# Down weights split by a converting and an adding transfer, and one weight sum of the seven products by an adding one

## The chip, the cores and the metric

The kernel runs on one NeuronCore of one Trainium2 chip. The metric is the device time of one launch in microseconds; lower is better. Five engines work side by side, each through its own queue, in order: TensorE (PE; its weight loads are listed as PEld), VectorE (DVE), ScalarE (ACT), GpSimd (POOL) and SyncE (SP). SP and POOL issue transfers, which run on 16 DMA engines.

## What is computed

A decoder trunk of two layers over 512 tokens and 16 learned ones, with 1024 features, in float32:

```
h = concat(meta, x)
for l in range(2):
    h = layer_norm(ALPHA * h + 0.5 * swiglu(h, ffn1_w_up[l], ffn1_w_down[l]))
    h = layer_norm(ALPHA * h + hybrid_mixer(h, ...))
    h = layer_norm(ALPHA * h + 0.5 * swiglu(h, ffn2_w_up[l], ffn2_w_down[l]))
return h[:, N_META:]

def swiglu(x, w_up, w_down):
    gate, up = jnp.split(x @ w_up, 2, axis=-1)      # 2 x 2816 columns
    return (jax.nn.silu(gate) * up) @ w_down
```

The mixer (a short convolution and an attention, gated) is not touched by the change.

## The kernel before

Each float32 product is made of three passes of a shorter format, float32r. An operand is split into hi (its value rounded to 12 significant bits) and lo (the exact rest); hi\*hi, hi\*lo and lo\*hi are summed in PSUM (`mm3`, lines 90 to 93). Weights are the stationary operand in up products and in most down products. So every tile of weights (128 x 1024 values, 512 KB) takes three steps ahead of its matmuls: SP loads it into a raw tile (`load`, line 105), ScalarE casts it to hi (line 111), and DVE subtracts to get lo (line 114). Line 111 and line 114 are in `operand`, which all weights share.

The pools that matter: `raw` has four buffers for raw tiles, `wp` four pairs hi and lo, and each feed-forward has a pool of its own (`dp` or `fp` in the code) with two buffers for raw tiles and two pairs hi and lo. A load waits until the last reader of its buffer is through.

There are four feed-forwards. Each starts with `up_start` (four tiles of features by plain products), which also makes four combinations of the tokens' parts (`combos`: POOL subtracts in line 337, ScalarE and DVE split in line 88). Then `up_seven` runs nine times, 36 times in the whole kernel. It makes two tiles of gate and two of up by seven products of halves, 24 matmuls each, in the order M1, M6, gate A, M7, M4, M5, M3. It reads four blocks of weights: g1, u1 and g2 into `raw`, u2 into the feed-forward's own pool, and makes further operands of them on DVE: S1 = u1 + u2 (line 431, into a tile of the own pool, where u2 lies too), S3 = g1 - u1 in u1's place (432), S2 = S1 - g1 in g1's place (433), S4 = g2 - S2 (441). M6 takes S2, M7 takes S3, M4 takes u2, M5 takes S1 and M3 takes S4, the last split in two halves on DVE. Products that share a bank of PSUM add to it: M6, M7 and M4 use one pair, and DVE reads it in between (lines 436, 446, 450); M5 and M3 use another (460, 468).

After M6 and after M5 stands one step of down products each (`steps`, line 498; two steps in the chunk that has one pair). A step makes one tile of down weights an operand in the feed-forward's own pool, where the two pairs hi and lo take turns, and multiplies it by the earlier chunk's activations for both halves of the tokens. DVE adds the results to the residual (line 558 in the first chunk, then 564, and 599 in the last feed-forward). In the first chunk of a feed-forward, DVE also converts the first features of each half of the tokens (line 253) and TensorE takes their mean (line 254, `shift_by`), which POOL subtracts (line 561). The weights of the last chunk go through `last_units` and not through `steps`.

The order of the instructions on an engine is not that of the source: in the trace, the sums and splits of the next `up_seven` stand between those of the present one, so that operands lie ready well ahead of their products.

Of the kernel before, what the change touches and what calls it, by code (L numbers as in the profile page):

```python
# [18 lines left out]
P = 128  # L19
# [18 lines left out]
# token ranges (first, width): all tokens, and those behind the meta tokens  # L38
FULL = ((0, 256), (256, 272))
TRIM = ((16, 256), (272, 256))  # L40
# and in two equal parts
EVEN = {FULL: ((0, 264), (264, 264)), TRIM: TRIM}
# chunks of the feed-forward features, in pairs of tiles
# [8 lines left out]
def trunk(ctx: ExitStack, tc: tile.TileContext, x, meta, f1_up, f1_dn, w_in, b_gate, conv_w, qn_g, w_uq,  # L52
          kvn_g, w_ukv, w_bc, w_bm, w_o, f2_up, f2_dn, ln_g, ln_b, rope, out):
    """Float32 products run as three passes of float32r: an operand is hi + lo, hi its value rounded to 12
    significant bits and lo the exact rest, and hi*hi + hi*lo + lo*hi are summed in PSUM. Activations lie with
    their features on the partitions."""
# [8 lines left out]
    @contextmanager  # L65
    def scratch(n, t):
        """The eight banks of PSUM, n for psum() and the others for psum2(), and t tiles in SBUF."""
        with tc.tile_pool(name="psp", bufs=1, space=bass.MemoryType.PSUM, reuse_waits="tile") as pool, \
                tc.tile_pool(name="tmp", bufs=t, reuse_waits="tile") as tp:
            banks.append((pool, n))  # L70
            tps.append(tp)
            yield
            banks.pop()
            tps.pop()
# [23 lines left out]
    def unit(pool=wp, k=8, c=P):  # L98
        """A stationary operand, hi and lo, as [128, k, c]."""
# [8 lines left out]
    def operand(raw, pool=wp, cut=1):  # L108
        """Split, in parts where others would wait for long."""
# [6 lines left out]

    def columns(src, c, pool=wp):
        """128 columns of a matrix with 1024 rows."""
        return operand(load(src[:, c:c + P], KD, P), pool)

# [10 lines left out]
    # per-feature parameters as columns  # L131
# [11 lines left out]
    def tokens_in(xt, c0):  # L143
        """Two tiles of tokens, to the columns from c0."""
# [14 lines left out]
    with tc.tile_pool(name="xload", bufs=1, reuse_waits="tile") as xp, scratch(4, 1):  # L159
# [8 lines left out]
        # the array's clock falls while it waits for the first products' operands: of no use but for that  # L168
# [3 lines left out]
    def rest_in(pool):  # L172
        """The other tokens, and the parameters."""
# [21 lines left out]
    # Per-token statistics are taken with the tokens on the partitions, n of them in each of nt columns, and  # L195
    # spread back over the partitions of the features.
# [5 lines left out]
    def token_sums(ps, at, parts, n, nt):  # L202
        """Columns at, at + 2, ...: the means over D features of the parts together."""
# [6 lines left out]
    def spread(c, n, nt, act, ps):  # L210
        """c / D on all partitions."""
# [10 lines left out]
    def rsqrt(v, n, nt, by=float(D)):  # L222
        """by/sqrt(v): the exponent trick, a Newton step, and a step of third order."""
# [13 lines left out]
    class Norm:  # L237
        """Layer norm over the features of r, which holds twice the sum to norm. The sums of r and of its squares
        are taken as its last parts come; by then r has been moved by a value near the mean of each token, which
        keeps the variance exact."""  # L240
# [7 lines left out]
        def shift_by(self, q0, w, i):  # L248
            """The mean of the first features of each token, on all partitions: near the mean, so that a rounded
            one does."""  # L250
# [22 lines left out]
        def run(self, q0, w):  # L273
            """The rest, in steps between which the tensor engine should have something else to do."""
# [44 lines left out]
    def project_steps(ps, u, nk, rhs, q0, w, n=4):  # L319
        """The same, with a stop after each n of the products' parts."""  # L320
# [7 lines left out]
    def combos(hv, th, tl):  # L328
        """Sums and differences of the parts of x (halves of its features, 1 and 2, and of its tokens, A and B)
        that the seven products take, split, from r that holds x. By index: T1 = x1B - x1A,  # L330
        T2 = x2B - T1, T3 = x2B - x1B, -T4 = x2A - T2."""
# [8 lines left out]
    def up_start(hp, dp, w_up, hv, pending, th, tl, after, begin):  # L340
        """silu(gate) * up for the first two pairs of feature tiles. What the first tokens allow comes first."""
# [857 lines left out]
```

## Time and profile before

| | |
|---|---|
| time, median of 3 runs | 2246.11 us (2245.96 to 2246.87) |
| span of the profiled execution | 2247.7 us |
| TensorE busy | 2202.0 us (98%) |
| DVE, ScalarE, POOL busy | 1679.5, 974.5, 372.6 us |
| TensorE clock granted, mean | 0.990 |
| transfers by SP's queue, by POOL's | 195.65 MB, 4.34 MB |

The span is that of one execution, from its first to its last instruction; no other time of that execution is given, so it is compared with the median of the runs. Busy time of an engine is time in which it has an instruction; idle time before an instruction is put down to what released it.

### The profile page before, as it was taken

To read this page: it belongs to the slowest core of one execution; us is meant where nothing else is said; L and a number is where in the kernel's file an instruction comes from. 1 tells how busy PE (TensorE), PEld (TensorE's weight loads), DVE (VectorE), ACT (ScalarE), POOL (GpSimd) and SP (SyncE) were. 2 spreads that over 40 slices of the span, in tenths; PEclk is the share of its full clock that TensorE was granted. 3 is DMA by queue.
4 is the path that set the end of the run, shared out by engine and by line. 5 is a ranking of instruction groups with operands and counts; after the bars stand their busy time and mean duration, and the time that the engine had idled before them with its cause. 6 is when DMAs were issued, how large, how long until landed. Compare 5 with 4: busy or idle time off the path is not lost. (4 is left out here: it accounts for less than half of the span.)

```text
span 2247.7 us, 43950 instructions
## 1 busy us (share of the span) xinstructions
PE 2202.0 (98%) x17989; PEld 2181.9 (97%) x17989; DVE 1679.5 (75%) x3191; ACT 974.5 (43%) x1881; POOL 372.6 (17%) x487
## 2 busy tenths in 40 slices
PE   9999999999999999999999999999999999999998
PEld 8999999999999999999999999999999999999998
DVE  6777778876646777878778778787665568877887
ACT  4343344465533543434353433444655335443441
POOL 3210004211014512000242100042110155100000
PEclk9999999999999999999999999999999999999999
DMA  5232232222233223323323232322222332233322
GB/s 172 94 103 91 90 119 77 68 62 67 69 92 104 66 82 98 113 75 111 107 66 95 96 98 90 113 85 63 66 67 76 94 94 85 76 103 105 99 90 86
DMA packets 237418, 202.80 MB, mean 90 GB/s; under 512 B 6990, under 2 KB 233360, under 8 KB 237216
## 3 DMA queue, kind: packets, MB, share of 16 engines
q1 hardware_dynamic: 234880, 195.65, 28.2%
q0 software_dynamic: 2336, 4.34, 0.7%
q8 instruction: 141, 2.31, 0.4%
q14 instruction: 61, 0.50, 0.1%
HBM read 195.74 MB, written 2.10 MB: 88 GB/s over the span
## 5 line engine op out<-in xcount | busy, mean ns | idle before, releaser
L114 DVE TENSOR_TENSOR wl<-raw,wh 128x1024 fp32r<-128x1024 f32 (+1 forms) x490 | 560.5, 1145 | 250.0 <-ACT wh L111 248.5
L111 ACT CAST wh<-raw 128x1024 fp32r<-128x1024 f32 (+1 forms) x454 | 466.2, 1034 | 591.2 <-PE ps L92 174.3
L92 PE MATMUL ps<-xl,wh 128*128 128x256 f32 (+2 forms) x1760 | 501.7, 285 | 2.7 <-DVE xl L88 2.7
L91 PE MATMUL ps<-xh,wh 128*128 128x256 f32 (+2 forms) x1760 | 502.5, 286 | 0.1
L93 PE MATMUL ps<-xh,wl 128*128 128x256 f32 (+2 forms) x1760 | 501.6, 285 | 0.0
L92 PEld LDWEIGHTS ps<-xl,wh 128*128 128x128 f32 x1760 | 332.5, 189 | 4.3 <-DVE xl L88 4.0
L91 PEld LDWEIGHTS ps<-xh,wh 128*128 128x128 f32 x1760 | 333.0, 189 | 0.6 <-ACT xh L88 0.5
L93 PEld LDWEIGHTS ps<-xh,wl 128*128 128x128 f32 x1760 | 333.4, 189 | 0.0
L91 PE MATMUL ps<-th,wh 128*128 128x264 f32 (+1 forms) x1152 | 328.5, 285 | 0.0
L92 PE MATMUL ps<-tl,wh 128*128 128x264 f32 (+1 forms) x1152 | 327.6, 284 | 0.0
L93 PE MATMUL ps<-th,wl 128*128 128x264 f32 (+1 forms) x1152 | 326.9, 284 | 0.0
L91 PE MATMUL pf<-hh,wh 128*128 128x256 f32 (+1 forms) x864 | 246.7, 286 | 0.0
L93 PE MATMUL pf<-hh,wl 128*128 128x256 f32 (+1 forms) x864 | 246.3, 285 | 0.0
L92 PE MATMUL pf<-hl,wh 128*128 128x256 f32 (+1 forms) x864 | 245.3, 284 | 0.0
L92 PEld LDWEIGHTS ps<-tl,wh 128*128 128x128 f32 x1152 | 218.8, 190 | 0.0
L91 PEld LDWEIGHTS ps<-th,wh 128*128 128x128 f32 x1152 | 218.6, 190 | 0.1
L93 PEld LDWEIGHTS ps<-th,wl 128*128 128x128 f32 x1152 | 218.3, 189 | 0.0
L91 PE MATMUL pf<-xh,wh 128*128 128x256 f32 (+1 forms) x640 | 188.0, 294 | 0.0
L92 PE MATMUL pf<-xl,wh 128*128 128x256 f32 (+1 forms) x640 | 184.4, 288 | 0.0
L93 PE MATMUL pf<-xh,wl 128*128 128x256 f32 (+1 forms) x640 | 183.2, 286 | 0.0
L91 PEld LDWEIGHTS pf<-hh,wh 128*128 128x128 f32 x864 | 162.7, 188 | 0.0
L93 PEld LDWEIGHTS pf<-hh,wl 128*128 128x128 f32 x864 | 162.7, 188 | 0.0
(323 smaller groups left out, 4870.3 us busy)
## 6 DMA issues: line engine op xcount, KB each, us to landing
raw<-in_ffn_w_up_dram SPq DMA_DIRECT2D x176, 512.0 KB, 3.6
raw<-in_ffn_w_down_dram SPq DMA_DIRECT2D x80, 512.0 KB, 3.3
raw<-in_mix_w_in_dram SPq DMA_DIRECT2D x64, 512.0 KB, 3.7
raw<-in_w_o_dram SPq DMA_DIRECT2D x16, 512.0 KB, 3.9
raw<-in_ffn_w_down_dram SPq DMA_DIRECT2D x16, 256.0 KB, 2.6
raw<-in_w_br_conv_dram SPq DMA_DIRECT2D x8, 512.0 KB, 3.3
raw<-in_w_br_mla_dram SPq DMA_DIRECT2D x8, 512.0 KB, 3.3
out_dram<-r SPq DMA_DIRECT2D x8, 256.0 KB, 2.4
```

What stands on the lines that cost most here:

```text
L91: PE.matmul(ps, lhsT=lhs[0], rhs=rhs[0], start=first, stop=False, skip_group_check=more)
L92: PE.matmul(ps, lhsT=lhs[0], rhs=rhs[1], start=False, stop=False, skip_group_check=more)
L93: PE.matmul(ps, lhsT=lhs[1], rhs=rhs[0], start=False, stop=last, skip_group_check=more)
L111: S.copy(u[0], raw)
L114: V.tensor_tensor(u[1][:, k:k + n], raw[:, k:k + n], u[0][:, k:k + n].bitcast(F32), op=ALU.subtract)
```

## The change

Down weights of `steps` no longer have a raw tile. POOL issues a transfer straight from DRAM that converts float32 to float32r into hi; ScalarE writes -hi into lo; POOL issues a second transfer of the same weights from DRAM that adds to lo. This holds for 80 tiles, 64 of 512 KB and 16 of 256 KB. In `up_seven`, S1 is made by a load of u1's block into S1's buffer (SP) and a transfer from u2 that adds to it (POOL), in place of DVE's line 431. The rest of the diff takes out comments.

```diff
+    def operand_dma(src, kc, cols, pool=wp):
+        u = unit(pool, kc, cols)
+        src = src.rearrange("(k p) c -> p k c", p=P)
+        G.dma_start(u[0], src)
+        S.activation(u[1], u[0].bitcast(F32), AF.Copy, scale=-1.0)
+        G.dma_start(u[1], src, accum_op=ALU.add)
+        return u
...
-        s1 = raw_tile(fp).rearrange("p (k c) -> p k c", c=256)
-        V.tensor_tensor(s1, u1, u2, op=ALU.add)          # S1
+        s1 = load(w_up[0:512, D_FF + f * P:D_FF + f * P + 256], KH, 256, fp)
+        G.dma_start(s1, u2, accum_op=ALU.add)
...
+            def weights_dma(ci, mp, pool):
+                f0, f1 = [2 * c for c in CHUNKS[ci]]
+                return operand_dma(w_dn[f0 * P:f1 * P, mp * 256:(mp + 1) * 256], f1 - f0, 256, pool)
...
-                        u = by_tile(operand(weights(ci, mp, rawp), dp), len(hs))
+                        u = by_tile(weights_dma(ci, mp, dp), len(hs))
```

## Rows read from the trace of the kernel before

**Rows 1.** The page, part 1: busy us, share of the span, instructions.

```profile
PE 2202.0 (98%) x17989; PEld 2181.9 (97%) x17989; DVE 1679.5 (75%) x3191; ACT 974.5 (43%) x1881; POOL 372.6 (17%) x487
```

**Rows 2.** Busy times by stretch; last columns PEclk, DMA share, GB/s; sum of four stretches.

```profile
1945.00:2200.00 255.00, 255.00 (x2165) 255.00 (x2164) 201.19 (x336) 100.97 (x157) 0.00 (x0) 1.00 0.30 96
sum 985.00, PE 985.00 PEld 984.82 DVE 769.73 ACT 385.94 POOL 33.47; mean PE 246.25 PEld 246.20 DVE 192.43 ACT 96.48 POOL 8.37
```

**Rows 3.** Timeline of PE, three stretches: start, duration, instruction, idle before, releaser.

```profile
79.84 0.41 PE L254 MATMUL ps<-t,onesb 128*128 128x272 bf16 x1 [2.67 <-DVE t L253]
...
829.84 0.29 PE L254 MATMUL ps<-t,onesb 128*128 128x272 bf16 x1 [2.38 <-DVE t L253]
...
1204.57 0.29 PE L254 MATMUL ps<-t,onesb 128*128 128x272 bf16 x1 [2.21 <-DVE t L253]
```

**Rows 4.** Busy times in slices of 1 us behind the second of these.

```profile
830.00:831.00 1.00, 1.00 (x7) 1.00 (x7) 0.00 (x0) 0.66 (x2) 0.37 (x1) 0.59 0.00 0
831.00:832.00 1.00, 1.00 (x7) 1.00 (x6) 0.20 (x1) 1.00 (x2) 1.00 (x2) 0.50 0.00 0
...
833.00:834.00 1.00, 1.00 (x8) 1.00 (x7) 0.46 (x2) 0.00 (x0) 0.00 (x0) 0.71 0.00 0
```

**Rows 5.** Timeline of DVE before the second stop of rows 3.

```profile
818.22 2.35 DVE L114 TENSOR_TENSOR wl<-raw,wh 128x1024 fp32r<-128x1024 f32 x2
...
822.76 0.29 DVE L253 CAST t<-r 128x256 bf16<-128x256 f32 x1
825.67 1.22 DVE L431 TENSOR_TENSOR raw<-raw 128x1024 f32<-128x1024 f32 x1 [2.62 <-DMA raw<-in_ffn_w_up_dram]
...
827.14 1.22 DVE L432 TENSOR_TENSOR raw<-raw 128x1024 f32<-128x1024 f32 x1
...
828.97 0.81 DVE L253 CAST t<-r 128x272 bf16<-128x272 f32 x1
```

**Rows 6.** Timeline of SP: the last of four loads, there and in a later `up_seven`.

```profile
820.61 0.37 SPq L105 DMA_DIRECT2D raw<-in_ffn_w_up_dram  x1
...
168.87 0.37 SPq L105 DMA_DIRECT2D raw<-in_ffn_w_up_dram  x1
```

**Rows 7.** DMA issues: count, KB each, median us from issue to landing.

```profile
raw<-in_ffn_w_down_dram SPq DMA_DIRECT2D x80, 512.0 KB, 3.3
...
wh<-in_ln_g_dram POOLq DMA_DIRECT2D x1, 512.0 KB, 3.9
wl<-in_ln_b_dram POOLq DMA_DIRECT2D x1, 512.0 KB, 5.2
```

**Rows 8.** Timeline of POOL: a transfer that it issues.

```profile
389.81 0.57 POOL L691 DMA_DIRECT2D cosT<-in_rope_dram  x1
```

**Rows 9.** Timeline of PE: gate A, M7, M3 and the next first step's product begin.

```profile
175.21 0.28 PE L91 MATMUL ps<-xh,wh 128*128 128x264 f32 x1
178.12 0.28 PE L91 MATMUL ps<-th,wh 128*128 128x264 f32 x1
...
192.71 0.28 PE L91 MATMUL ps<-xh,wh 128*128 128x264 f32 x1
...
201.47 0.28 PE L91 MATMUL pf<-hh,wh 128*128 128x256 f32 x1
```

**Rows 10.** Timeline of ACT in the same `up_seven`: two of its casts of weights.

```profile
178.25 1.05 ACT L111 CAST wh<-raw 128x1024 fp32r<-128x1024 f32 x1 [1.00 <-PE ps L92]
...
184.36 2.00 ACT L111 CAST wh<-raw 128x1024 fp32r<-128x1024 f32 x2 [2.16 <-DMA raw<-in_ffn_w_down_dram]
```

**Rows 11.** Timeline of DVE in the same `up_seven`.

```profile
179.34 0.69 DVE L114 TENSOR_TENSOR wl<-raw,wh 128x512 fp32r<-128x512 f32 x1 [3.42 <-ACT wh L111]
179.94 0.43 DVE L446 TENSOR_TENSOR t<-ps,t 128x264 f32<-128x264 f32 x1
...
183.72 1.22 DVE L433 TENSOR_TENSOR raw<-raw 128x1024 f32<-128x1024 f32 x1
...
187.40 0.77 DVE L460 TENSOR_TENSOR t<-ps,t 128x264 f32<-128x264 f32 x2
```

## The prediction

> **What bounds the kernel now.** I read first the page's busy times: TensorE is busy 2202.0 of the span's 2247.7 us [rows 1], so an edit that gives no matmul less can win 45.7 us at most. Then the busy times by stage: in the middle of the four feed-forwards (985 us together) TensorE is busy all the time at full clock, with DVE busy for 201.2 us of the 255 in the stretch shown [rows 2]. That is where nearly all of the edited instructions stand, so relief of DVE buys nothing there, whatever it amounts to.
>
> Third, TensorE's timeline, for the idle time that the edit can reach. In three of the four feed-forwards TensorE stops once, in the first `up_seven`, before the second matmul of `shift_by` (line 254): 2.67, 2.38 and 2.21 us, released by DVE's line 253 [rows 3]. After each the granted clock stands at its lower level, 1.2 GHz instead of 2.4: 0.59, 0.50, 0.50 (the slice not shown is like 831) and 0.71 in four 1-us slices, which loses 0.41 + 0.50 + 0.50 + 0.29 = 1.70 us of full-clock time [rows 4]; the other two have the same pattern. The fourth feed-forward has no `shift_by`. DVE's timeline shows why line 253 is late: after the first one (822.76 to 823.05) DVE waits 2.62 us for a load of `w_up`, does line 431 (the sum S1) for 1.22 us, and only then the rest: 432, the residual's 558, and 253 at 828.97 [rows 5]. The load was issued as the last of four on SP's queue, at 820.61 [rows 6], right after the two splits on DVE that began at 818.22 and took 2.35 us [rows 5]; so its buffer was freed by the second of them. In a later `up_seven` the last of the four is likewise issued at 168.87 [rows 6]. `u2` and S1 share the feed-forward's own pool of two, the others lie in the pool of four; I take the last load to be `u2`.
>
> **The change, part by part.**
>
> *S1 (36 times).* DVE loses line 431: 36 x 1.22 us [rows 5]. At the three stops this is on the path. Line 432 (S3) takes g1 and u1, not `u2`, so DVE no longer waits for the last load. What DVE has left behind 823.05 is 558 for two parts of the residual, 432 (1.22) and 253: with 1.14 us to the next start for 431 and the 2.62 us wait gone, 253 comes 3.76 us earlier, at 825.2 instead of 828.97, and the stop began at 829.84 - 2.38 = 827.46 [rows 3, 5]. The stop goes. Bounds for one stop: above, all of it with its low clock; below, only the 1.14 us of 431 if the wait stays; both if u1 is the late load. I take the upper end, as the last issue follows a split that frees `u2`'s pool. Sum: 2.67 + 2.38 + 2.21 = 7.26 us, and 3 x 1.70 = 5.1 us of clock: 12.4 us.
>
> In exchange S1 is late: SP loads u1's block a second time into S1's buffer, and POOL issues an adding transfer from `u2`. In the ordinary `up_seven`, `u2` is issued at 168.87; a load of 512 KB lands 3.3 us after its issue [rows 7], so a second one behind it can land at about 176. The adding one has no row. Nearest is a 512 KB load issued by POOL, 3.9 and 5.2 us [rows 7], with an issue of 0.57 us [rows 8]. Below, I bound it by 3.9; above, by three times 5.2 = 15.6, as it reads the sum too. I take 7.8 (half more than 5.2: three streams where a load has two). It lands at 176 + 0.6 + 7.8 = 184.4, and line 433, its first reader, runs at 183.72 now [rows 11]: DVE waits 0.7 us. What is behind 433 on DVE is up A, its split, and line 460, which empties the bank that M3 adds to from 192.71 [rows 9]. Some 3.7 us lie between the starts of 433 and 460 (183.72 and 187.40) [rows 11], so S1 may land as late as 189.0. Cost: nothing; without that cover, 36 times the excess.
>
> *Down weights (80 times, 64 of them 512 KB).* DVE loses its split and SP a load; ScalarE's cast becomes a copy with a factor at the same size, taken at the cast's 1.05 us [rows 10]. POOL gets two transfers each, one that converts and one that adds. The buffers hi and lo are free when the last but one down product ends. For the first of the two steps of an `up_seven` that is 175.21, and its next product begins at 201.47 [rows 9]: 26.3 us. The chain: issue 0.57; converting transfer 5.2 (bounds 3.9 and twice 5.2); ScalarE 1.05; issue 0.57; adding transfer 7.8 (bounds 3.9 and 15.6): 15.2 us, between 10.0 and 28.2. At 15.2 it is hidden with 11 us to spare; it would cost only if both transfers together took over 24.1 us, where I take 13.0. ScalarE now waits for the converting transfer in its own queue, and behind it stand the casts of the next operands; they are some 14 us ahead of their products (the cast at 178.25 is for M3 at 192.71) [rows 9, 10]. ScalarE waited 2.16 us for the down load already, at 184.36 [rows 10], and TensorE did not feel it. Cost: nothing, unless it is ahead of the cast at 178.25 (below).
>
> *POOL and the transfers.* POOL issues 5 transfers of some 0.57 us [rows 8] in one `up_seven`. It takes them in order: the one that adds lo waits for ScalarE's copy, and behind it stand S1's, the next converting one and, in the first chunk, the residual's subtractions (line 561). Each has over 10 us before its reader but S1, which is costed above; so nothing. By bytes, six loads in an `up_seven` become seven, and three adding transfers with three streams come on top: the DMA share of 0.30 [rows 2] becomes some 0.30 x (7 + 4.5) / 6 = 0.58. The pool of raw tiles, four deep, keeps three tiles of an `up_seven` instead of three and the two of down; loads can only start earlier for that.
>
> The traffic at the stops is where rule and row must be weighed. A load of down weights takes 3.3 us in the median [rows 7]; the last of these four loads takes 825.67 - 820.61 = 5.1 [rows 5, 6]: transfers in flight together slow each other, by some 1.8 us here. The Trainium skill (DMA: Bandwidth & Descriptors, "Issuing engines are not separate DMA queues") says that transfers from SP, ACT and POOL run on the same 16 engines and interleave; by that rule the second load of u1's block is added to the batch, whichever queue it has. The traces agree as far as SP's queue goes. By the row for `u2` alone the sum is 12.4; with the rule it is rival 1.
>
> **The sum.** 12.4 us less, nothing more: 2247.7 - 12.4 = 2235.3 for the profiled execution, whose span is 1.6 us above the median of the runs, 2246.11; so 2233.7 by the median.
>
> **Rivals.**
>
> 1. *The stop only shrinks, or another wait takes its place.* u1 is the last to land, or the added transfers slow it by the 1.8 us seen above; then 1.14 us per stop come off, or less, and the low clock stays: 3.4 us at most, 2242.7 to 2247. For: it is not in the rows which load came last, and the order of each engine's queue can come out otherwise. Against: the buffer's pool. Chance 0.20.
>
> 2. *ScalarE's wait stands ahead of the cast for M3 (slower).* The buffers are free at 175.21 and the cast starts at 178.25 [rows 9, 10]. If the copy of -hi is queued before that cast, the cast waits for the landing, 175.21 + 0.57 + 5.2 = 181.0, and the copy, 1.05: 182.0. DVE's half split at 179.34 waits for the cast and line 446 at 179.94 stands behind it [rows 11]; 446 empties the bank into which M4 adds from about 181.0 (M7 began at 178.12 and takes 2.9). So 446 ends 3.75 us late, at 184.1, TensorE stops for 3.1 us, and the low clock takes up to 1.7 more: 36 times 3.1 to 4.8, 2358 to 2419. In a few of the 36 only, 2255 to 2300. It decides from a landing after some 178 in that order; in the other order never. Against: the copy can be planned only for when its transfer is due, over 3 us after 175.21 if that takes the 3.9 of [rows 7], which is after 178.25. Chance 0.18.
>
> 3. *The adding transfer is slow.* Beyond 12.4 us (landing after 189) DVE holds up line 460 and M3. At the bound, 15.6, that is 3.2 us a time, 36 times: 2361, more with the clock; at 13 us, 2268. For: no row shows an adding transfer. Against: it takes 2.4 times the slower POOL load. Chance 0.17.
>
> That the change does not do what it says (the sum still waits on DVE for the same load) is rival 1's case.
>
> **How the numbers follow.** Forecast (both parts hidden, the stops gone) 0.45; rival 1, 0.20; rivals 2 and 3 together 0.35. A measurement of this kernel tells 0.2% (4.5 us) from no change. Faster by more is the forecast, 0.45; rival 1 lies within 0.2%; the other two are slower. The forecast's own range is 2231 (a little of the last feed-forward's wait goes too) to 2241. The full range reaches through rival 1 into the milder half of rivals 2 and 3, to 2300: 0.45 + 0.20 + 0.16, with 0.19 left out above.
>
> **What would show it.** Right: no idle time of TensorE at line 254 and full clock around it; 432 on DVE with no wait for a load; all four middle stretches still busy throughout; converting and adding transfers near 5 and 8 us. Wrong: idle time at M4 behind 446 with ScalarE waiting for the converting transfer (rival 2); DVE waiting at 433 for an adding transfer and TensorE at M3 (rival 3); lo landing after its down product is due.

## The result and the profile after

The changed kernel takes 2396.42 us (median of four runs, 2390.86 to 2402.14) where the kernel before takes 2246.49: ratio 1.0669, interval 1.0651 to 1.0687. It is 150 us slower; the prediction was 2233.7 us, with 2300 us as the upper end. The profiled execution has a span of 2400.4 us.

In the lines that follow, the code has moved: 253/254 became 263/264, 432 became 442, 433 became 443, 441 (S4) became 451, 446 became 456, 460 and 468 became 470 and 478, 371 became 381, 564 became 578, 337 became 347, 617 became 631. Line 122 is the converting transfer, 123 the copy of -hi, 124 the adding transfer for lo, 441 the adding transfer for S1.

First the page: busy times (to be read against [rows 1]), DMA queues, and DMA issues with the median time from issue to landing ([rows 7]).

```profile
PE 2244.5 (94%) x17989; PEld 2213.0 (92%) x17989; DVE 1550.3 (65%) x3075; ACT 969.3 (40%) x1881; POOL 547.9 (23%) x683
...
q1 hardware_dynamic: 215744, 176.77, 24.3%
q0 software_dynamic: 83808, 98.73, 22.4%
...
raw<-in_ffn_w_up_dram SPq DMA_DIRECT2D x212, 512.0 KB, 4.7
wh<-in_ffn_w_down_dram POOLq DMA_DIRECT2D x64, 512.0 KB, 5.0
wl<-in_ffn_w_down_dram POOLq DMA_DIRECT2D x64, 512.0 KB, 6.1
...
raw<-raw POOLq DMA_DIRECT2D x36, 512.0 KB, 4.9
```

DVE has lost 129 us of work, and TensorE, with the same 17989 matmuls, is busy 42.5 us longer. Busy times by stretch, in two feed-forwards (columns as in [rows 2]: length, busy time of PE, PEld, DVE, ACT and POOL with their instructions, then PEclk, DMA share, GB/s):

```profile
200.00:300.00 100.00, 86.07 (x664) 84.78 (x664) 57.10 (x103) 32.43 (x51) 16.89 (x17) 0.95 0.56 124
...
2200.00:2300.00 100.00, 93.02 (x760) 92.21 (x759) 61.48 (x112) 33.23 (x53) 17.32 (x18) 0.97 0.66 151
```

In the kernel before, these places lie in the stretches of [rows 2], with TensorE busy throughout at clock 1.00; TensorE now stops in them, and the clock is lower. The waits (engine, what it was to write, the releaser: us in total, times, longest) name what ended the stops, and what the other engines waited for:

```profile
PE ps L91 <- DVE t L456: 32.1, 14, 4.3
PE ps L91 <- DVE t L478: 27.1, 12, 2.5
PE ps L91 <- DVE t L470: 22.1, 22, 2.4
PE ps L91 <- DVE t L381: 15.9, 3, 5.4
PE pf L91 <- DVE r L578: 14.4, 3, 5.9
...
DVE wl L114 <- ACT wh L111: 453.8, 162, 10.1
DVE raw L442 <- DMA raw<-in_ffn_w_up_dram: 52.7, 27, 5.3
...
DVE raw L443 <- DMA raw<-raw: 8.0, 6, 2.1
...
ACT wl L123 <- DMA wh<-in_ffn_w_down_dram: 221.6, 47, 15.4
...
POOL wl L124 <- ACT wl L123: 226.1, 38, 10.3
POOL raw L441 <- DMA raw<-in_ffn_w_up_dram: 162.3, 24, 11.1
...
SPq L105 <- DVE raw L451: 559.0, 34, 32.5
```

Two of these in the kernel before:

```profile
DVE wl L114 <- ACT wh L111: 248.5, 230, 4.7
...
SPq L105 <- DVE raw L441: 220.7, 32, 22.2
```

The sum can be closed. All of TensorE's waits in this view come to 144.2 us in 86 stops, against 35.0 us in 35 stops before: 109.2 us. With 42.5 us more of busy time, which is the same matmuls at a lower granted clock (mean 0.975, before 0.990), that makes 151.7 us of the 152.7 us between the spans. So the loss is stops of TensorE and the lower clock around them, and nearly all the stops (133.3 of the 144.2 us, 72 of the 86) were ended by DVE, which has *less* to do than before. DVE is late because it waits: 453.8 us for ScalarE's casts (before 248.5).

How one such stop comes about is seen in the timeline of one `up_seven` (start, duration, engine, line, tiles, and in brackets the idle time before and its releaser):

```profile
229.64 0.88 POOL L441 DMA_DIRECT2D raw<-raw  x1 [8.76 <-DMA raw<-in_ffn_w_up_dram]
230.19 1.10 POOL L122 DMA_DIRECT2D wh<-in_ffn_w_down_dram  x1
...
236.66 1.06 ACT L123 ACTIVATE wl<-wh 128x1024 fp32r<-128x1024 f32 x1 [14.93 <-issue]
...
237.89 1.04 ACT L111 CAST wh<-raw 128x1024 fp32r<-128x1024 f32 x1
238.01 1.28 POOL L124 DMA_DIRECT2D wl<-in_ffn_w_down_dram  x1 [6.72 <-ACT t L453]
...
238.96 0.69 DVE L114 TENSOR_TENSOR wl<-raw,wh 128x512 fp32r<-128x512 f32 x1 [5.87 <-ACT wh L111]
239.57 0.43 DVE L456 TENSOR_TENSOR t<-ps,t 128x264 f32<-128x264 f32 x1
...
240.05 0.39 PE L91 MATMUL ps<-th,wh 128*128 128x264 f32 x1 [1.63 <-DVE t L456]
```

Read it downwards. POOL stands 8.76 us at S1's adding transfer, because the second load of u1's block has not landed. The converting transfer is right behind it in the queue and goes out 0.55 us later. Its tile lands 6.4 us after its issue, at 236.6; ScalarE has by then been idle for 14.93 us (the view names no releaser for this wait, but the copy starts as the tile lands) and takes the copy of -hi first, since that stands first in its queue; the cast for M3 comes after. DVE waits for that cast, and line 456, which empties the bank that M4 adds to, stands behind on DVE. TensorE stops for 1.63 us. An `up_seven` earlier, at 192.13, and one before that, at 154.27, POOL shows the same pair of lines after waits of 9.54 us (ended, by the profile, by a split on DVE) and 8.88 us. In the whole trace there are 17 such pairs: S1's transfer waits 8.4 to 12.2 us, and the converting one goes out 0.55 us later with no wait of its own. The casts and sums on this chain are not at fault; one transfer that had to wait on POOL holds up a transfer that did not, and three in-order queues pass it on.

The stops at line 478 (27.1 us in 12) have another last step. Just ahead of the chain above, DVE shows S3 waiting for u1's load, with line 478 behind it, and TensorE waiting for that:

```profile
215.66 1.23 DVE L442 TENSOR_TENSOR raw<-raw 128x1024 f32<-128x1024 f32 x1 [2.69 <-DMA raw<-in_ffn_w_up_dram]
...
217.63 0.39 PE L91 MATMUL ps<-th,wh 128*128 128x264 f32 x1 [2.46 <-DVE t L478]
```

That load was issued at 212.03, when S4 on DVE (210.72) had freed its buffer.

What did go as predicted: line 264 (before 254) on TensorE, by source line.

```profile
L264 PE MATMUL ps<-t,onesb x10: 269/276/283, 82.9 to 1946.9; 128*128 128x256 bf16 x6, 128*128 128x272 bf16 x4
its engine sat idle before it (us, times) until:
who waited for it (us, times):
```

Nothing stands under "sat idle before it": the three stops of [rows 3] are gone.

### The profile page after: what moved, and what is told of

Its sections match the earlier page's. It is cut to its first block, busy times and chain, and to the rows that moved or that the text cites. A ratio compares the mean times of both kernels' runs of the same rounds, so it can differ in the third digit from the quotient of the medians.

```text
span 2400.4 us, 44203 instructions
## 1 busy us (share of the span) xinstructions
PE 2244.5 (94%) x17989; PEld 2213.0 (92%) x17989; DVE 1550.3 (65%) x3075; ACT 969.3 (40%) x1881; POOL 547.9 (23%) x683
## 3 DMA queue, kind: packets, MB, share of 16 engines
q1 hardware_dynamic: 215744, 176.77, 24.3%
q0 software_dynamic: 83808, 98.73, 22.4%
## 5 line engine op out<-in xcount | busy, mean ns | idle before, releaser
L114 DVE TENSOR_TENSOR wl<-raw,wh 128x1024 fp32r<-128x1024 f32 (+1 forms) x410 | 470.4, 1149 | 454.6 <-ACT wh L111 453.8
L111 ACT CAST wh<-raw 128x1024 fp32r<-128x1024 f32 x374 | 389.8, 1047 | 335.4 <-PE ps L92 134.3
L91 PE MATMUL ps<-th,wh 128*128 128x264 f32 (+1 forms) x1152 | 336.9, 292 | 59.2 <-DVE t L456 32.1
L92 PE MATMUL ps<-tl,wh 128*128 128x264 f32 (+1 forms) x1152 | 333.3, 289 | 0.0
L93 PE MATMUL ps<-th,wl 128*128 128x264 f32 (+1 forms) x1152 | 332.8, 289 | 0.0
L91 PE MATMUL pf<-hh,wh 128*128 128x256 f32 (+1 forms) x864 | 252.8, 293 | 14.4 <-DVE r L578 14.4
L92 PEld LDWEIGHTS ps<-tl,wh 128*128 128x128 f32 x1152 | 224.7, 195 | 0.0
L93 PEld LDWEIGHTS ps<-th,wl 128*128 128x128 f32 x1152 | 224.3, 195 | 0.0
L124 POOL DMA_DIRECT2D wl<-in_ffn_w_down_dram x80 | 102.2, 1277 | 438.0 <-ACT wl L123 226.1
L123 ACT ACTIVATE wl<-wh 128x1024 fp32r<-128x1024 f32 (+1 forms) x80 | 77.7, 972 | 275.9 <-DMA wh<-in_ffn_w_down_dram 221.6
```

The costliest lines, as they stand in the source:

```text
L91: PE.matmul(ps, lhsT=lhs[0], rhs=rhs[0], start=first, stop=False, skip_group_check=more)
L92: PE.matmul(ps, lhsT=lhs[0], rhs=rhs[1], start=False, stop=False, skip_group_check=more)
L93: PE.matmul(ps, lhsT=lhs[1], rhs=rhs[0], start=False, stop=last, skip_group_check=more)
L111: S.copy(u[0], raw)
L114: V.tensor_tensor(u[1][:, k:k + n], raw[:, k:k + n], u[0][:, k:k + n].bitcast(F32), op=ALU.subtract)
L123: S.activation(u[1], u[0].bitcast(F32), AF.Copy, scale=-1.0)
```

## The experiments

All ratios are to the kernel before, timed beside it on the same chip. The order of every queue is planned anew when a kernel is built, so a price below is that of the edit with the order that comes with it. How much the order changed can be counted in the traces. Without S1's adding transfer, and without lo's, it is nearly that of the changed kernel: TensorE's and SP's are the same, and of DVE's 3075 and ScalarE's 1881 instructions 6 and 3 stand elsewhere (4 and 4 without lo's). With the down weights alone, TensorE's is the same too. With hi ahead of S1, 169 and 62 stand elsewhere; with S3 later, 849 and 226. What TensorE's waits and its busy time grow by accounts for the longer span within 3 us in every one. In the expectations, Q is the theory that in-order queues hand on a wait (ScalarE's in the first three, POOL's with it from then on), R that the raw buffers take turns otherwise, P that the plan's places do it. T and S, in the first three, are that the transfers are too slow and that S1 is late for S2.

| kernel | time, us | ratio (interval) | PE waits, us (stops) | PE busy, us |
|---|---|---|---|---|
| S1 alone | 2251.3 | 1.0031 (1.0020 to 1.0042) | 38.8 (41) | 2199.1 |
| down weights alone | 2271.7 | 1.0116 (1.0101 to 1.0131) | 53.4 (43) | 2205.2 |
| both (the change) | 2396.4 | 1.0669 (1.0651 to 1.0687) | 144.2 (86) | 2244.5 |
| -hi by POOL | 2413.9 | 1.0748 (1.0728 to 1.0768) | 154.0 (73) | 2241.0 |
| S3 later | 2346.5 | 1.0454 (1.0429 to 1.0480) | 103.3 (80) | 2227.7 |
| S1 added by POOL | 2314.5 | 1.0301 (1.0281 to 1.0321) | 87.9 (62) | 2214.4 |
| no adding for lo | 2326.5 | 1.0367 (1.0350 to 1.0384) | 90.8 (71) | 2221.1 |
| hi alone by transfer | 2297.1 | 1.0228 (1.0212 to 1.0244) | 72.4 (50) | 2210.8 |
| hi ahead of S1 on POOL | 2308.4 | 1.0263 (1.0230 to 1.0295) | 82.1 (57) | 2215.6 |
| no adding for S1 | 2274.3 | 1.0133 (1.0117 to 1.0149) | 60.8 (43) | 2207.0 |
| sums reordered, no transfer changed | 2234.7 | 0.9952 (0.9937 to 0.9967) | 30.0 (37) | 2194.6 |

### One part at a time

S1's part alone, with the down weights as before; then the down weights alone, with S1 by DVE:

```diff
-                        u = by_tile(weights_dma(ci, mp, dp), len(hs))
+                        u = by_tile(operand(weights(ci, mp, rawp), dp), len(hs))
```

> Only S1 by the adding transfer; down weights as before (raw tile, ScalarE's cast, DVE's split). Theory Q (in-order queues: POOL holds the converting transfer behind S1's adding one, ScalarE's copy waits for it, and the casts behind the copy make DVE and TensorE late): nothing on ScalarE waits for POOL here, so the loss of 150 us is gone and the three stops at the second matmul of shift_by too: 2234 to 2243 us. Theory T (the transfers themselves are too slow, 16 engines at 0.6 busy): S1's share of the added bytes is about a third, so some 50 us of the loss stay: about 2295. Theory S (S1 is late for line 433, everything else follows): the loss stays nearly whole, 2350 or more.

```diff
-        s1 = load(w_up[0:512, D_FF + f * P:D_FF + f * P + 256], KH, 256, fp)
-        G.dma_start(s1, u2, accum_op=ALU.add)
+        s1 = raw_tile(fp).rearrange("p (k c) -> p k c", c=256)
+        V.tensor_tensor(s1, u1, u2, op=ALU.add)
```

> Only the down weights by transfers; S1 by DVE as before. Theory Q: POOL has no S1 ahead of the converting transfer, which is then issued when its buffer is free, some 5 us earlier than in the changed kernel; ScalarE still waits for it, 5.0 us less what passes before the copy's turn: a part of the loss stays, 2255 to 2320 us, with ScalarE's waits before the copy clearly under the 221.6 us of the changed kernel. Theory T: two thirds of the loss stay, about 2345. Theory S: the loss is gone, 2235 to 2250.

2251.3 and 2271.7 us: 6 and 26 us over the kernel before, where both together cost 150. S1 alone misses Q's 2234 to 2243 by some 8 us, the down weights alone lie in Q's range, and T and S are out. Neither part is much of the loss; 118 us are their interaction. In TensorE's waits of S1 alone, the three stops are gone and others have come:

```profile
PE ps L91 <- DVE t L456: 8.8, 5, 2.5
PE ps L91 <- DVE t L470: 3.6, 5, 1.3
```

In the waits of the down weights alone:

```profile
PE ps L91 <- DVE t L381: 15.6, 3, 5.3
...
PE pf L631 <- DVE t L629: 8.1, 1, 8.1
PE ps L91 <- DVE t L456: 7.4, 11, 1.3
```

Its waits are 18.4 us longer than before, and the starts of the four feed-forwards make all of that: 15.6 us in three, and in the fourth 8.1 us before a transpose of the residual (line 631; 3.4 us before). The prediction never costed them. The traces show what holds up the four. At the start of a feed-forward POOL makes the tokens' combinations (line 347, 337 before). With the down weights alone, the first converting transfer waits on POOL for its buffer, and the combinations stand behind it. At the third start, first in this kernel, then in the kernel before:

```profile
1183.69 0.79 POOL L122 DMA_DIRECT2D wh<-in_ffn_w_down_dram  x1 [21.24 <-DVE wl L114]
...
1186.25 0.78 POOL L347 TENSOR_TENSOR t<-r 128x264 f32<-128x264 f32 x1
```

```profile
1152.08 0.96 POOL L337 TENSOR_TENSOR t<-r 128x264 f32<-128x264 f32 x1
```

The last combination follows at 1199.74, where it was at 1181.95 before. ScalarE's casts of the combinations wait for POOL, DVE's splits follow them, and line 381 (629 at the fourth start) stands behind the splits: TensorE stops 5.22 us, until 1203.40. At the four starts this first transfer waits 43.5, 20.5, 21.2 and 19.4 us. So these stops, too, are a transfer that waits on POOL ahead of work that does not; no run tests that by itself.

### Is it ScalarE's place in the chain?

The copy of -hi moved to POOL:

```diff
-        S.activation(u[1], u[0].bitcast(F32), AF.Copy, scale=-1.0)
+        G.tensor_scalar(u[1], u[0].bitcast(F32), -1.0, None, op0=ALU.mult)
```

> The changed kernel with -hi written by POOL instead of ScalarE, so that only POOL waits for the converting transfer; the same transfers, the same bytes. Theory Q: ScalarE's casts are on time again, the loss goes but for what POOL's own queue holds up: 2235 to 2270 us. Theory T: nothing changes, 2380 to 2420. Theory S: little changes, as S1 still comes by the adding transfer: 2350 or more.

2413.9 us, not faster. ScalarE no longer waits for the converting transfer, and TensorE now waits for lo itself and, as before, for DVE:

```profile
PE pf L93 <- DMA wl<-in_ffn_w_down_dram: 36.7, 10, 6.7
PE ps L91 <- DVE t L478: 32.5, 12, 6.5
```

So Q's 2235 to 2270 us for this run was wrong: taking the wait off ScalarE is no cure. The run does not part ScalarE's share from POOL's, since the copy takes 2.8 us on POOL (median, 1.06 on ScalarE) in the very queue where the transfers stand.

### Is it the turn of the raw buffers?

With three raw tiles in a block and four buffers, the load of u1 waits for S4 of the block before (SP's line with L451 above, 559.0 us; before 220.7), and S3, planned soon behind S4 on DVE, waits for that load (52.7 us). Two kernels take a raw tile more for each step, to make the buffers turn as before; the second also loads 1 KB into it.

```diff
                 f0, f1 = [2 * c for c in CHUNKS[ci]]
+                raw_tile()
                 return operand_dma(
```

> The changed kernel with one raw tile more taken from the shared pool, and never used, for each group of down weights, so that the pool's four buffers turn as they did before. Theory R (turn of the buffers): with three raw tiles in a block and four buffers, u1 of a block gets the buffer that g1 held in the block before; its load leaves only when S4 has read that one (SyncE waited 559 us for S4 in the changed kernel, 220.7 us before), and S3, next behind S4 on VectorE, waits for the landing (52.7 us in 27 waits) with the whole VectorE queue behind it. Then SyncE's wait for S4 falls to about 220 us, S3's wait below 30 us, and the time to 2250-2300 us. Theory Q (POOL's queue: an adding transfer that waits holds up the converting one behind it): POOL's queue is as it was, and the time stays at 2370-2400 us.

> The kernel with the down weights' transfers alone (S1 by VectorE, 2271.7 us), with the same unused raw tile for each group of down weights. Theory R: S1's wait for the up loads (76.7 us in 32 waits) falls to the 37.4 us of the kernel before, and the time to 2240-2258 us. Theory Q: nothing of POOL's queue is changed, and the time stays at 2265-2280 us.

2397.6 and 2275.3 us, both as without it; SP's wait for S4 stayed at 561.1 us, so a tile that nobody uses took no buffer, and the two say nothing.

```diff
+                nc.sync.dma_start(raw_tile()[0:1, 0:256], w_dn[f0 * P:f0 * P + 1, mp * 256:(mp + 1) * 256])
                 return operand_dma(
```

> The changed kernel with a raw tile of the shared pool taken for each group of down weights and one row of 1 KB loaded to it by SyncE, which nothing reads: the unused tile of the run before took no buffer (SyncE's wait for S4 stayed at 561.1 us), this one does. Theory R (turn of the four buffers): u1's load no longer waits for S4 of the block before; SyncE's wait for S4 falls to 200-300 us, S3's wait for u1 (52.7 us) below 25 us, the time to 2290-2350 us. Theory Q (POOL's and ScalarE's queues): POOL's waits for the negated copy and for the second load stay as they are, and the time at 2370-2400 us.

2373.8 us, 1.0551 (1.0531 to 1.0570):

```profile
SPq L105 <- DVE raw L451: 382.7, 34, 29.4
```

SP's wait did shrink, but S3's stayed (51.3 us in 26 waits), and the time lies in Q's range. Half undone, the turn of the buffers gives about 1% of the time. The small loads wait on SP's queue themselves, so this is no clean test; that the turn alone is not the loss is better seen with the down weights alone, where SP waits 429.1 us for S4 and the time is 2271.7.

### S3 and S1 later on DVE

S3 is queued behind the last split of the block before; then the same with the copy on POOL; then S1 in that place in the kernel with the down weights alone, and in the kernel before.

```diff
-        V.tensor_tensor(u1, g1, u1, op=ALU.subtract)
+        with tc.issue_after(last_split[-1].ins) if last_split else nullcontext():
+            V.tensor_tensor(u1, g1, u1, op=ALU.subtract)
```

> The changed kernel with S3 queued on VectorE behind the last split of the block before, so that it no longer stands right behind S4; nothing else is changed by hand. Theory R: what costs is that VectorE's queue stands still behind S3; S3's wait for the load of u1 (52.7 us in 27 waits) falls below 15 us and the time to 2290-2340 us. Theory Q: POOL's and ScalarE's waits (226 us for the negated copy, 222 us for the converted tile) are as they were, and the time stays at 2370-2400 us.

> The changed kernel with S3 later on VectorE's queue (alone: 2346.5 us) and the negated copy on POOL instead of ScalarE (alone: 2413.9 us). With S3 later the tensor engine still waited 42.3 us, in 32 stops, for ScalarE's cast, which stands behind the negated copy. If those are what ScalarE's place costs, they go, and the time falls to 2290-2325 us. If POOL's queue is what holds things up (it becomes 3 us longer for each group), the time stays at 2340 us or rises, to 2400 us.

> The kernel with the down weights' transfers alone (2271.7 us) with S1 queued on VectorE behind the last split of the block before. If its 26 us are VectorE's wait for the up loads at S1 (76.7 us in 32 waits), that wait falls below 20 us and the time to 2245-2258 us. If they come from POOL's queue and the starts of the feed-forwards (15.6 us at the combinations and 8.1 us at the last norm), the time stays at 2262-2280 us.

> The kernel before with nothing but S1 queued on VectorE behind the last split of the block before. If the wait of S1 for the up loads (37.4 us in 26 waits) costs the tensor engine nothing but the three stops before the squares (12.4 us with the low clock behind them), the time is 2234-2246 us. If S1's later place makes S2 and the operand of M6 late, the time rises by 5 us or more, to 2250-2290 us.

The first gives 2346.5 us: 50 us less, and S3's wait for u1 falls from 52.7 to 1.4 us; the 12 stops at line 478 are gone. A third of the loss goes with S3's place and the other order that comes with it; the rest stays, and part of it has only moved, to the casts on ScalarE:

```profile
PE ps L91 <- ACT wh L111: 42.3, 32, 4.9
```

With the copy on POOL as well it is 2354.0 us (1.0475; 1.0449 to 1.0501), no better. S1 in the later place makes both other kernels slower: 2324.4 us (1.0341; 1.0325 to 1.0357) instead of 2271.7, and 2266.5 us (1.0080; 1.0065 to 1.0095) instead of 2247.2. The latter was expected; for the former neither range held (2245 to 2258, 2262 to 2280). A later place helped S3, but not S1, though S1 too waited for its load with the down weights alone (76.7 us).

### S1 without its two transfers, and without the adding one

S1 by POOL's own adder, no second load:

```diff
-        s1 = load(w_up[0:512, D_FF + f * P:D_FF + f * P + 256], KH, 256, fp)
-        G.dma_start(s1, u2, accum_op=ALU.add)
+        s1 = raw_tile(fp).rearrange("p (k c) -> p k c", c=256)
+        G.tensor_tensor(s1, u1, u2, op=ALU.add)
```

> The changed kernel with S1 added by POOL itself (u1 + u2, about 3 us an instruction) in place of the second load and the adding transfer. If it is the second load and the adding transfer's way through DRAM (a load more on SyncE's queue, 4.9 us more before S2) that costs, the time falls to 2260-2300 us, near the 2271.7 us of the kernel with the down weights' transfers alone. Theory Q: POOL still waits for u2 with the down weights' transfers behind, and the time stays above 2360 us. Theory R: the turn of the buffers is as in the changed kernel, S3 still waits about 50 us for u1, and the time is 2340-2390 us.

2314.5 us. S3 now waits for POOL, since it overwrites u1:

```profile
DVE raw L442 <- POOL raw L441: 156.0, 33, 6.1
```

That is three times the wait for u1's load in the changed kernel, and yet 82 us less time. So idle time of DVE at S3 is not the measure of the loss. Nor is the waiting on POOL: S1 stands ahead of a converting transfer in all 36 blocks here and waits 288.8 us for loads (162.3 in the changed kernel), ScalarE waits 217.6 us for hi, and the loss is less than half. None of the three ranges held. (No DRAM lies on the adding transfer's own way: HBM reads grow from 195.7 to 252.4 MB with the change, which is the second loads and lo's second reads.) Then the second load alone, with its adding transfer taken out:

```diff
-        G.dma_start(s1, u2, accum_op=ALU.add)
```

> The changed kernel without S1's adding transfer: the second load of u1's block stays, S1 is that load alone, so the sum of S1 is left out. Theory Q (POOL's queue: the adding transfer waits up to 11 us for the second load and the converting transfer behind it starts late): POOL's queue holds only the down weights' transfers, and the time falls to 2265-2300 us. Theory P (the places that the planner gave to S3 and to the loads on SyncE, which stay as they are): S3's wait for u1 stays near 50 us, and the time is 2340-2400 us.

2274.3 us, the time of the down weights alone (2271.7) within their intervals. The second load on SP's queue, the longer batch, the turn of the buffers (SP waits 447.2 us for S4 here) are all still there, and cost nothing to speak of. The 36 adding transfers for S1 carry 122 of the 150 us, in a plan that is nearly the same, as Q expected; P is out. S3 stands where it stood, but waits 27.8 us for u1 instead of 52.7, and the stops at line 478 are gone: POOL's wait reaches that branch too. (By which way is argued, not tested: S4, which frees u1's buffer, stands on DVE behind splits that wait for ScalarE's casts.) Its waits:

```profile
ACT wl L123 <- DMA wh<-in_ffn_w_down_dram: 138.1, 53, 10.9
...
POOL wh L122 <- PE pf L93: 459.1, 62, 20.3
```

POOL's converting transfer now waits for what it should, the last reader of its buffer on TensorE, and ScalarE's wait for hi falls from 221.6 to 138.1 us.

### The other half of the ring

The waits above close a ring: POOL waits for a load, the load for S4 on DVE, DVE for ScalarE's casts, ScalarE for the transfer that POOL holds. The same from the side of the down weights: without their adding transfer (lo stays -hi), and with hi alone by a transfer, lo by DVE from a raw tile.

```diff
-        G.dma_start(u[1], src, accum_op=ALU.add)
```

> The changed kernel without the down weights' adding transfer: their lo stays the negated hi, so lo's exact rest is left out; the converting transfer, the negated copy and both of S1's transfers stay. Theory Q, in the half that POOL waits for ScalarE's copy (226 us in 38 waits) and holds S1's adding transfer and the next converting one behind it: the time falls to 2270-2320 us. If it is ScalarE's wait for the converting transfer (221.6 us) with the casts behind it, the time stays at 2350-2395 us.

```diff
-        src = src.rearrange("(k p) c -> p k c", p=P)
-        G.dma_start(u[0], src)
-        S.activation(u[1], u[0].bitcast(F32), AF.Copy, scale=-1.0)
-        G.dma_start(u[1], src, accum_op=ALU.add)
+        raw = load(src, kc, cols)
+        G.dma_start(u[0], src.rearrange("(k p) c -> p k c", p=P))
+        V.tensor_tensor(u[1], raw, u[0].bitcast(F32), op=ALU.subtract)
```

> The changed kernel with the down weights' lo taken by VectorE from a raw tile that SyncE loads, as before, and hi by the converting transfer; no negated copy and no adding transfer for them. ScalarE waits for no transfer of theirs and POOL for no ScalarE. If the chain over three engines (converted tile, negated copy, adding transfer) is what couples the queues, the time is 2246-2275 us, near the 2251.3 us of S1's transfers alone. If S1's adding transfer ahead of the converting one is enough, the time is 2300-2390 us.

2326.5 us, 70 less than the change, just above the first range (2270 to 2320), with ScalarE's wait for hi not less, at 239.0 us. So lo's adding transfers matter too, by POOL's wait at them (226.1 us in the changed kernel) or by their traffic; this run does not part the two. And since hi is as late here, and in the kernel with S1 added by POOL, as in the changed one, at about half the loss, a late hi alone does not set the price. 2297.1 us with hi alone, which is 46 us over S1 alone (2251.3); neither expectation of 2246 to 2275 us nor of 2300 and more is quite met. Some 22 us of its stops are again the starts of feed-forwards (17.4 and 8.1, where S1 alone has 3.4 in all), and DVE itself now waits 84.6 us for the converting transfer, so the run does not say what S1's adding transfer ahead of a converting one costs by itself.

### Only the place on POOL

In 24 of the 36 blocks the planned queue of POOL has S1's adding transfer right ahead of a converting one, in the other 12 right behind one. This kernel keeps every transfer and puts S1's behind the first converting one of its block in all 36 (in 7 it then stands ahead of the next):

```diff
-        G.dma_start(s1, u2, accum_op=ALU.add)
+        mid[0].start()
+        with tc.issue_after(hi[-1].ins):
+            G.dma_start(s1, u2, accum_op=ALU.add)
...
+                def start():
+                    first[mps[0]] = hi_only(ci, mps[0], dp)
```

> The changed kernel with S1's adding transfer always queued on POOL behind the converting transfer of the block's first group of down weights (it stood right ahead of one in 24 of 36 blocks). Theory Q1, taken narrowly (the converting transfer is late because it stands behind the adding one that waits): ScalarE's wait for the converting transfer falls from 221.6 us to below 160 us, near the 138.1 us without the adding transfer, and the time to 2270-2330 us. If the adding transfer costs wherever it stands, since lo or the next S2 then waits behind it, the time stays at 2350-2400 us.

2308.4 us: 88 of the 150 us are gone, as expected (2270 to 2330), with every transfer still there; the edit is to the order of one queue, though the plan moved some instructions of DVE and ScalarE as well (169 and 62, above). So the traffic of S1's adding transfers is not the main part of their 122 us. The waits (ScalarE's for hi; then what is left; 122 is the copy here, 380 and 459 are the change's 381 and 456):

```profile
ACT wl L122 <- DMA wh<-in_ffn_w_down_dram: 130.0, 45, 10.1
...
DVE raw L446 <- DMA raw<-raw: 51.4, 19, 6.7
...
PE ps L91 <- DVE t L380: 21.8, 5, 7.5
PE ps L91 <- DVE t L459: 16.0, 11, 2.4
```

In POOL's timeline of this kernel the converting transfer (line 512 here) goes out first, the adding one (444) behind it:

```profile
181.41 0.77 POOL L512 DMA_DIRECT2D wh<-in_ffn_w_down_dram  x1 [6.14 <-PE pf L93]
183.58 0.88 POOL L444 DMA_DIRECT2D raw<-raw  x1 [1.40 <-DMA raw<-in_ffn_w_up_dram]
```

ScalarE's wait is at the level without the adding transfer (138.1); the price now is paid by S1, which S2 (line 446 here) waits for 51.4 us, where it was 8.0. What remains over the down weights alone is 37 us.

### The stops without any transfer

The three stops come from S1 being first on DVE and needing u2. The sums can be made in another order, S3 = g1 - u1, S2 = u2 - S3, S1 = S2 + g1, in the kernel before and in the one with the down weights alone:

```diff
-        V.tensor_tensor(s1, u1, u2, op=ALU.add)          # S1
         V.tensor_tensor(u1, g1, u1, op=ALU.subtract)     # S3
-        V.tensor_tensor(g1, s1, g1, op=ALU.subtract)     # S2
+        V.tensor_tensor(s2, u2, u1, op=ALU.subtract)     # S2
+        V.tensor_tensor(g1, s2, g1, op=ALU.add)          # S1
```

> The kernel before, no transfer changed, with the weight sums in another order: S3 = g1 - u1 first, then S2 = u2 - S3, then S1 = S2 + g1. The first of them no longer needs u2, whose load is the last of the four, so VectorE's wait at S1 (37.4 us) shrinks below 15 us, and if the three stops before the squares go with it (12.4 us with the low clock), the time is 2232-2244 us. If S1 in g1's buffer holds that buffer longer and the loads start later, the time rises to 2250-2290 us.

> The kernel with the down weights' transfers alone (2271.7 us) and the sums in the other order (S3 = g1 - u1, S2 = u2 - S3, S1 = S2 + g1). If its 26 us are mostly VectorE's wait at S1 for u2 (76.7 us in 32 waits), the time falls by 10 us more than the other order gave alone, to 2235-2250 us. If they are POOL's transfers behind buffers and the starts of the feed-forwards (15.6 us and 8.1 us), it falls by 10 us at most, to 2258-2272 us.

2234.7 us, ratio 0.9952 (0.9937 to 0.9967): faster than both kernels. Its waits, where the line before had 7.3 us in 3:

```profile
PE ps L254 <- DVE t L253: 2.2, 3, 0.9
```

TensorE's waits fall by 5.0 us and its busy time by 7.4, together the 12.4 us between the two profiled spans (2247.7 and 2235.3); between the medians it is 10.5 us, 7 to 14 by the interval. DVE still waits 26.5 us for loads at S3 (37.4 at S1 before), so the expected 15 us was missed, with no harm. With the down weights by transfers it is 2267.4 us (1.0089; 1.0070 to 1.0107), only 4 us less than without the new order: the 26 us of that part are not S1's wait (76.7 us at S1, 19.2 at S3 in the new order). The stops at the starts are there as before (15.9 and 8.1 us).

## Why the prediction was wrong

*The stops (12.4 us less): right.* Line 442 no longer waits for `u2`, and nothing waits before line 264. The reordered sums show the size by themselves, 10.5 us between medians. That the two profiled spans differ by 12.4 us, the prediction's very sum, is luck: they are made of 5.0 us of stops and 7.4 of busy time, where the prediction had 7.3 and 5.1.

*Sizes of the transfers: near, or on the safe side.* The converting one takes 5.0 us in the median (taken at 5.2), lo's adding one 6.1 and S1's 4.9 (7.8); the DMA share is 0.56 and 0.66 in the two stretches (0.58). POOL's issues are longer than [rows 8] gave: 0.78 us in the median for the converting one, 0.87 for S1's and 1.27 for lo's instead of 0.57, though the next can start before one has ended (0.55 us behind S1's). Rival 3, the slow adding transfer, did not happen: DVE waits only 8.0 us for S1's sum in the changed kernel. S1's own step, "Cost: nothing", was off by a little: alone, S1's part gave the three stops back and still came out 6 us above the kernel before, with 12.4 us of new stops at lines 456 and 470.

*The step that failed* is "Each has over 10 us before its reader but S1, which is costed above; so nothing", the step on POOL's queue. It weighed each transfer against its own reader, and listed what stands behind which, but gave no time to the waiting itself. S1's adding transfer cannot be issued before the second load lands. The prediction had that load at "about 176", 7 us after `u2`; in the changed kernel SP's loads stand behind u1, whose buffer comes free with S4, and POOL waited 162.3 us in 24 cases and up to 11.1 us in one for the load. Meanwhile the converting transfer behind it was not issued; in 17 blocks it then went out with no wait of its own, after 8.4 to 12.2 us of S1's. The 26.3 us of cover that the down weights had [rows 9] were counted from the time that the buffers come free, with nothing ahead in the queue. Taking out the waiting transfer gave 122 us back, and moving it behind 88, the latter with some change of the other queues. The list of what stands behind also lacked the combinations (line 337 before): behind the first converting transfer of a feed-forward they cost most of the 26 us of the down weights alone, by the traces. What stays open is why the same hold on POOL costs less than half when POOL adds S1 itself.

*"Loads can only start earlier for that"* failed as well, at a smaller size: without the two down tiles in between, u1 gets the buffer that S4 reads last, and SP's wait for S4 grew from 220.7 to 559.0 us. Half undone, that gave 23 us of the 150; S3 later on DVE gave 50, with the stops at line 478.

*"Cost: nothing, unless it is ahead of the cast at 178.25", and rival 2.* Rival 2 had the path and its price: the cast for M3 behind the copy of -hi, DVE's half split behind the cast, line 446 (456 now) behind that, TensorE stopped at M4. That is the chain in the timeline at 229 to 240 us, and the largest of the stops (32.1 us in 14). Its full size was 2358 to 2419 us; the measured 2396 lies in it, but by another sum: 51 more stops at several lines, mean wait 2.1 us, and 0.8 us of low clock for each (42.5 / 51), instead of one long stop at M4 in each of the 36. It was set aside with "the copy can be planned only for when its transfer is due". That the copy stands ahead of the cast in ScalarE's queue is seen in the timeline; why the plan has it there is not. With S1's adding transfer out of POOL's queue, ScalarE's order is the same but for 3 instructions and the copy still waits 138.1 us for hi, and TensorE loses only 28 us; what turned the order on ScalarE into stops is S1's adding transfer on POOL's queue. The range ended at 2300 because it left out the severe half of rivals 2 and 3, with a chance of 0.19, and the result lies there. The two were each priced alone; nowhere did the prediction ask what the two edits do to each other on the one queue that they share.

*The cap.* That relief of DVE buys nothing was right: 129 us less of DVE work bought nothing that these runs show but the three stops, and those can be had for no transfer at all.

*Rule and row.* The Trainium skill (DMA: Bandwidth & Descriptors, "Issuing engines are not separate DMA queues") says that transfers of several issuers interleave on the same 16 engines. The trace agrees: the up loads of SP, 3.6 us in the median before, take 4.7 in the changed kernel. It decided little here: with all that traffic but S1's adding transfers, up loads at 4.4 us, the time is 2274.3 us.

## What to carry to other kernels

A transfer that has to wait for another one (an adding transfer, above all) is a wait placed on the issuing queue: before moving work to it, write down that queue's order with the time at which each entry *may* go, and let every later entry, the queue's own arithmetic with it, start no earlier than the ones ahead. Price two edits that share an in-order queue together, not one by one; here 6 and 26 us made 150. The waits in total do not give the price: kernels with as much of them on POOL and ScalarE lost about half. And look at the order of the arithmetic before moving it: the sum that waited for the last load was simply the wrong one to take first.

## What the runs showed of the hardware

An adding transfer from SBUF to SBUF of 512 KB lands 4.9 us after its issue, one from DRAM 6.1, a converting one from DRAM 5.0, beside 4.7 for the plain loads of SP in the same execution. The packets of the adding transfers for lo are the dear ones: POOL's queue carries 98.73 MB in 22.4% of the 16 engines' span, and 60.97 MB in 11.8% without them (page of the kernel that leaves them out, span 2323.5 us). So, as an estimate from these two executions, their 37.8 MB took some 263 us of the 16 engines' time, 7.0 us for each MB, where SP's queue takes 3.3 (24.3% of 2400.4 us for 176.77 MB): an adding transfer from DRAM costs the engines about twice what a load does.
